# A two-layer hybrid encoder: down products of the second tokens held back, two token-major pairs, a third weight buffer set, and other places for the weight splits

## The chip, the cores and the metric

The kernel runs on one core of one Trainium2 chip. The metric is the device time of one execution in microseconds; what is compared is the median of several runs. One execution was also recorded by the hardware profiler; its page and its trace are what the text reads. The engines are called PE (TensorE, matrix products; its weight loads are shown apart as PEld), DVE (VectorE), ACT (ScalarE), POOL (GpSimd) and SP (SyncE, which here only issues DMAs).

## The reference

Two layers act on 256 tokens of width 1024 in float32. Each layer adds three sub-layers to the residual stream x, each with an RMS norm before it (pre) and after it (post):

```
for l in range(DEPTH):                                    # DEPTH = 2
    h = rmsnorm(x, ffn1_pre_g[l])
    x = x + 0.5 * rmsnorm(swiglu(h, ffn1_w_gate[l], ffn1_w_up[l], ffn1_w_down[l]), ffn1_post_g[l])
    h = rmsnorm(x, mix_pre_g[l])
    x = x + rmsnorm(hybrid_mixer(h, w_in[l], w_out[l], ...), mix_post_g[l])
    h = rmsnorm(x, ffn2_pre_g[l])
    x = x + 0.5 * rmsnorm(swiglu(h, ffn2_w_gate[l], ffn2_w_up[l], ffn2_w_down[l]), ffn2_post_g[l])

def swiglu(h, w_gate, w_up, w_down):
    return (silu(h @ w_gate) * (h @ w_up)) @ w_down       # 1024 -> 2816 -> 1024
```

The mixer projects h to 4 groups of heads (gated DeltaNet, differential attention, Mamba-2 SSD, mLSTM), and w_out maps their 1024 joined columns back. The change leaves the inside of the mixer as it is, apart from where weights lie.

## The kernel before, in words

**Six phases.** `phases` runs f1, mix, f2 of layer 0 and then of layer 1. Between two phases stands `boundary` (L512); one opens the first phase, one ends the last.

**Exact products from rounded parts.** Each float32 operand is split into hi (rounded by an ACT copy) and lo (a DVE subtraction), and a product is three matmuls: hi·hi, hi·lo, lo·hi. So each weight tile is loaded by SP as `raw` (L299), rounded by ACT into `hi` (L170) and subtracted by DVE into `lo` (L321). All weights of the program stand in one list, `stream`, in the order of use; it is worked through in halves of 512 KB. `split_to(n)` splits all halves up to n, `load_to` issues their loads, and `weights(i, ahead)` splits up to entry i plus `ahead` halves. There are 4 raw buffers and 8 split buffers, 4 in the pools `whi`/`wlo` ("w") and 4 in `ehi`/`elo` ("ext"); `room` says which half goes where, and `shifted` which are put 32 columns into their buffer. The mixer takes the place of "ext" while it runs.

**A feed-forward phase.** The 2816 columns are 11 pairs of 256 (`NPAIR`). For a pair, `project_T` computes gate and up transposed (weights stationary, all 256 tokens moving; 48 matmuls each), `swish` and `split_h` make the two parts of the hidden block, and two pairs later `contract` adds that pair's down product to four PSUM banks, one for each token half t (128 tokens) and output half h; each call is 6 matmuls of 512 columns. So a step of the loop is 96 matmuls of 256 columns and 24 of 512. The first pair of a phase is computed token-major by `ffn_first` (tokens stationary, `project`), so that it can start as soon as the 128 tokens of t = 0 are normed; its hidden block is turned by 4 transposes (`ps_hT`).

**The boundary.** For each t, `Norm` does: sum of squares of the bank (`junk_acc`, ACT), times the post gain (`ny`, DVE), the root (`rms_tail`: two small ACT and three small DVE instructions), the residual update (`x`, two DVE instructions), the sum of squares of x (`junk_x`), times the pre gain (half on DVE, half on POOL), the second root, the scaling (`ny`, DVE and ACT), 8 transposes (`flip`, PE, tile `ps_xT`), and the split into `xhi` and `xlo`. After t = 0 comes the first token-major work on t = 0, then the same chain for t = 1. All down products (or, after the mixer, all output products: `finish`) are issued before the boundary begins. The order is written out by hand (`manual_schedule`), and each engine works through its instructions in that order.

**The opening.** x, the identity, the first pre-norm gain spread over 128 partitions (512 KB, `gain_row`, L341) and the first weights are loaded, and the norms run without a post part.

## Time and profile before

| | before |
|---|---|
| median of 3 runs | 1195.69 us (1194.63 to 1198.77) |
| profiled execution | 1197.52 us, its span 1195.7 us |
| PE busy | 1120.7 us (94%) |
| DVE, ACT, POOL busy | 754.8, 580.2, 60.8 us |
| granted PE clock, mean | 0.970 |
| DMA | 189.64 MB, mean 159 GB/s |

The span runs from the first to the last recorded instruction; the execution's own time is 1.8 us longer. A busy share is an average over the phases, so it is read by place: in a steady loop an engine is either the bound or not, and at a boundary the question is which wait ends last. In the rows of the timeline the first number is the start and the second the duration in us; "idle before" names what the instruction waited for. In the rows by stretch come the length, then the busy time of each engine, the granted clock of PE, the share of the DMA engines and GB/s.

### The profile page before, as it was taken

What the parts mean: (1) busy time and instruction counts of PE and PEld (TensorE: products, weight loads), DVE (VectorE), ACT (ScalarE), POOL (GpSimd) and SP (SyncE); (2) the same over time, 40 slices, a digit from 0 to 9 for tenths busy, and PEclk for the clock granted to TensorE, in tenths of its full rate; (3) what the DMA queues carried; (4) which work ended last, traced back from release to release, by engine and by line L of the source; (5) the groups of instructions that cost most, each with busy time, mean ns of one, the idle gap of its engine ahead of it and who ended that gap; (6) DMA issues with size and microseconds to landing.
All of it is one profiled execution on the core that took longest, in us unless ns stands there. A gap on an engine that the chain in (4) does not pass through costs nothing.

```text
span 1195.7 us, 20955 instructions
## 1 busy us (share of the span) xinstructions
PE 1120.7 (94%) x8468; PEld 1039.9 (87%) x8468; DVE 754.8 (63%) x1306; ACT 580.2 (49%) x953; POOL 60.8 (5%) x76
## 2 busy tenths in 40 slices
PE   5999998999979889999989999989999798999997
PEld 4999897899968789999889999978998687999996
DVE  4655546877777865555476555477777677655535
ACT  5544536534344564544465444355335446544434
POOL 1000000010201000000000000001012010000000
PEclk9999999989989999999989999989899898999999
DMA  7866556322325466666447656454214243766642
GB/s 233 290 214 194 179 156 179 107 64 78 107 71 176 139 215 188 182 195 210 144 157 230 188 180 197 143 143 126 73 51 142 72 148 119 248 208 199 189 141 71
DMA packets 148851, 189.64 MB, mean 159 GB/s; under 512 B 12190, under 2 KB 133266, under 8 KB 148626
## 3 DMA queue, kind: packets, MB, share of 16 engines
q1 hardware_dynamic: 148754, 188.31, 50.4%
q8 instruction: 66, 1.08, 0.4%
q14 instruction: 31, 0.25, 0.1%
HBM read 187.24 MB, written 1.05 MB: 157 GB/s over the span
## 4 chain that ended last, share of the span: by engine, by line
PE 72%; DVE 11%; ACT 7%; DMA 6%; issue 3%; SPq 0%; POOL 0%; DVEq 0%; ACTq 0%
PE pgu L196 33%; PE acc L196 16%; DMA raw_d<-in_ffn_w_down 2%; PE ps_dq L196 2%; DMA raw_g<-in_ffn_w_gate 2%; PE ps_av L196 1%; PE ps_s L196 1%; PE ps_y L196 1%; PE ps_bq L196 1%; PE ps_dv L196 1%; PE ps_do L196 1%; PE ps_aq L196 1%; ACT hi_g L170 1%; PE ps_cz L196 1%; PE ps_ak L196 1%
## 5 line engine op out<-in xcount | busy, mean ns | idle before, releaser
L196 PE MATMUL pgu<-xhi,hi_g 128*128 128x256 f32 x640 | 178.4, 279 | 6.8 <-DVE hf L176 6.8
L196 PE MATMUL pgu<-xlo,hi_g 128*128 128x256 f32 x640 | 178.2, 278 | 0.0
L196 PE MATMUL pgu<-xhi,lo_g 128*128 128x256 f32 x640 | 177.9, 278 | 0.0
L196 PE MATMUL pgu<-xhi,hi_u 128*128 128x256 f32 x640 | 177.1, 277 | 0.0
L196 PE MATMUL pgu<-xhi,lo_u 128*128 128x256 f32 x640 | 176.9, 276 | 0.0
L196 PE MATMUL pgu<-xlo,hi_u 128*128 128x256 f32 x640 | 176.8, 276 | 0.0
L321 DVE TENSOR_TENSOR lo_u<-raw_u,hi_u 128x1024 fp32r<-128x1024 f32 x88 | 107.2, 1224 | 77.9 <-ACT hi_u L170 72.9
L321 DVE TENSOR_TENSOR lo_d<-raw_d,hi_d 128x1024 fp32r<-128x1024 f32 x88 | 104.6, 1222 | 64.1 <-ACT hi_d L170 63.5
L170 ACT ACTIVATE hi_u<-raw_u 128x1024 fp32r<-128x1024 f32 x88 | 92.7, 1060 | 95.6 <-PE pgu L196 87.2
L196 PE MATMUL acc<-hi_d,mlo 128*128 128x512 f32 x352 | 138.8, 394 | 0.0
L196 PE MATMUL acc<-lo_d,mhi 128*128 128x512 f32 x352 | 138.0, 392 | 0.0
L321 DVE TENSOR_TENSOR lo_g<-raw_g,hi_g 128x1024 fp32r<-128x1024 f32 x88 | 104.2, 1222 | 52.1 <-ACT hi_g L170 52.0
L196 PE MATMUL acc<-hi_d,mhi 128*128 128x512 f32 x352 | 136.8, 389 | 0.0
L196 PEld LDWEIGHTS pgu<-xhi,hi_g 128*128 128x128 f32 x640 | 120.7, 189 | 8.9 <-DVE hf L176 7.6
L196 PEld LDWEIGHTS pgu<-xlo,hi_g 128*128 128x128 f32 x640 | 120.8, 189 | 1.6
L196 PEld LDWEIGHTS pgu<-xhi,lo_g 128*128 128x128 f32 x640 | 120.9, 189 | 0.0
L196 PEld LDWEIGHTS pgu<-xhi,hi_u 128*128 128x128 f32 x640 | 120.2, 188 | 0.0
L196 PEld LDWEIGHTS pgu<-xlo,hi_u 128*128 128x128 f32 x640 | 120.1, 188 | 0.0
L196 PEld LDWEIGHTS pgu<-xhi,lo_u 128*128 128x128 f32 x640 | 120.1, 188 | 0.0
L170 ACT ACTIVATE hi_g<-raw_g 128x1024 fp32r<-128x1024 f32 x88 | 88.9, 1055 | 53.5 <-issue 36.9
L170 ACT ACTIVATE hi_d<-raw_d 128x1024 fp32r<-128x1024 f32 x88 | 88.9, 1049 | 52.3 <-PE pgu L196 34.1
L176 DVE TENSOR_TENSOR hf<-pgu,sg 128x256 f32<-128x256 f32 x88 | 36.8, 422 | 74.3 <-ACT sg L142 74.1
(494 smaller groups left out, 2355.7 us busy)
## 6 DMA issues: line engine op xcount, KB each, us to landing
raw_g<-in_ffn_w_gate SPq DMA_DIRECT2D x88, 512.0 KB
raw_u<-in_ffn_w_up SPq DMA_DIRECT2D x88, 512.0 KB
raw_d<-in_ffn_w_down SPq DMA_DIRECT2D x88, 512.0 KB
raw_wo<-in_w_out SPq DMA_DIRECT2D x16, 512.0 KB
raw_s<-in_w_in SPq DMA_DIRECT2D x4, 528.0 KB
g_ffn_pre_g<-in_ffn_pre_g SPq DMA_DIRECT2D x4, 512.0 KB
g_ffn_post_g<-in_ffn_post_g SPq DMA_DIRECT2D x4, 512.0 KB
raw_cz<-in_w_in SPq DMA_DIRECT2D x4, 512.0 KB
```

What stands on the lines that cost most here:

```text
L170: return nc.scalar.activation(out=out, in_=in_, func=AF.Copy, **kw)
L176: return (eng or V).tensor_tensor(out=out, in0=a, in1=b, op=op)
L196: return nc.tensor.matmul(out, lhsT=lhsT, rhs=rhs, start=start, stop=stop)
L321: V.tensor_sub(out=lo, in0=raw[:, 0:m], in1=hi.bitcast(F32))
```

## The change

1. **Down products held back.** In the loop the down products of pairs 7 and 8 (those of the last two steps) are done for t = 0 only. After the loop come pairs 9 and 10 for t = 0. The rest for t = 1 is passed to `boundary` as `tail`: pairs 7 and 8, and 9 and 10 for h = 0, are issued at its start (36 matmuls), pairs 9 and 10 for h = 1 (12 matmuls) after the transposes of t = 0. After the mixer the same is done with the output products of t = 1 (12 and 12).
2. **Two token-major pairs.** In all feed-forward phases but the first, `ffn_first` does pairs 0 and 1. At the boundary three of t = 0's four blocks (24 matmuls each) stand before the transposes of t = 1 and one behind; t = 1's four blocks follow. There are 8 transposes of hidden blocks in place of 4.
3. **Buffers.** A third set of 4 split buffers ("x2", pools `xhi`/`xlo`) exists outside the mixer, and there are 6 raw buffers in place of 4. `ROLES` gives each phase its sets for even pairs, odd pairs and down weights. The columns of the buffers, the paddings and `shifted` change with them, and the mixer's weights are no longer shifted.
4. **Places for splits.** Within a feed-forward phase splits run 6 halves ahead but not into the next phase. The first halves of the next phase are split before the boundary (4 between two feed-forward phases and before the mixer of layer 0, none before the mixer of layer 1, 2 after a mixer), and others at five points inside it (`fills`): around the residual update of t = 0, after its scaling, between the two halves of t = 1's post part, around t = 1's update, and after its scaling.
5. **Norms.** Both halves of x times the pre gain are on DVE, each behind its half's sum of squares; POOL has no part in it.
6. **The opening.** The first gain is loaded as one row of 4 KB into one partition and spread by two float32 matmuls with a row of ones; the norms read it from PSUM. The weight splits of the first pair are placed between the steps of the norms.

The core of the diff:

```diff
+RAW = 6
+AHEAD = 6
+ROLES = {(0, "f1"): ("w", "x2", "ext"), (0, "f2"): ("x2", "w", "ext"), (1, "f1"): ("x2", "ext", "w"), (1, "f2"): ("x2", "w", "ext")}
...
+    tpad = ctx.enter_context(tc.tile_pool(name="tpad", bufs=1))
+    tpad.tile([128, 104], F32, name="tskew")
...
-            nh = 2 * (len(stream) - c0)
+            shifted.update(2 * ids[l, st, "u", m] for m in range(1, NPAIR))
+            even, odd, down = ROLES[l, st]
             for m in range(NPAIR):
-                for nm in "gu":
-                    shifted.add(2 * ids[l, st, nm, m] + (m == 0))
-            for j in range(nh):
-                if j >= nh - 4:
-                    more = True
-                elif j >= nh - 6:
-                    more = False
-                else:
-                    more = j // 4 % 2 == 1
-                room[2 * c0 + j] = "ext" if more else "w"
+                where = odd if m % 2 else even
+                for nm in "gud":
+                    i = ids[l, st, nm, m]
+                    room[2 * i] = room[2 * i + 1] = where if nm != "d" else odd if m >= NPAIR - 2 else down
...
-                if n != "ak":
-                    shifted.add(2 * ids[l, n] + (n in ("cz", "do", "bv", "dv")))
...
+    def split_hi():
+        n = len(parts)
+        load_to(n + RAW - 1)
+        w, k2, _, name, _ = half_of(n)
+        m = w * k2
+        where = room.get(n)
+        if isinstance(where, tuple):
+            hi, lo = (ph.pools["early"].tile([128, 1024], F32R, tag=g, name=h + name) for g, h in zip(where, ("hi_", "lo_")))
+        elif where in ("ext", "x2"):
+            a, b = ("ehi", "elo") if where == "ext" else ("xhi", "xlo")
+            hi = ph.pools[a].tile([128, 1088], F32R, tag="hi", name="hi_" + name)
+            lo = ph.pools[b].tile([128, 1088], F32R, tag="lo", name="lo_" + name)
+        else:
+            hi = hip.tile([128, WMAX], F32R, tag="hi", name="hi_" + name)
+            lo = lop.tile([128, WMAX], F32R, tag="lo", name="lo_" + name)
+        o = 32 if n in shifted else 0
+        acopy(hi[:, o:o + m], raws[n][:, 0:m])
+        half_done.append((hi[:, o:o + m], lo[:, o:o + m]))
+    def split_lo():
+        n = len(parts)
+        w, k2, _, name, _ = half_of(n)
+        hi, lo = half_done.pop()
+        V.tensor_sub(out=lo, in0=raws[n][:, 0:w * k2], in1=hi.bitcast(F32))
+        parts.append(tuple(a.rearrange("p (k f) -> p k f", k=k2) for a in (hi, lo)))
+        load_to(n + RAW)
...
+    def weights(i, ahead=0, limit=NHALF):
+        split_to(max(2 * i + 1, min(2 * i + 1 + ahead, limit - 1)))
...
+    def first_gain_load(name, l):
+        V.memset(sall[0:1, 0, 0:128], 1.0)
+        nc.sync.dma_start(out=flat(npbd[0:1]), in_=t_in[name][l].rearrange("(o n) -> o n", o=1))
+
+    def first_gain():
+
+        ps = [psg("ps_gain%d" % h) for h in range(2)]
+        for h in range(2):
+            mm(ps[h][:], sall[0:1, 0, 0:128], flat(npbd[0:1])[:, 512 * h:512 * h + 512])
+        return ps
...
-            mul(self.y[:, HALF[0]], xt[t][:, HALF[0]], self.gpre[:, HALF[0]])
-            mul(self.y[:, HALF[1]], xt[t][:, HALF[1]], self.gpre[:, HALF[1]], eng=G)
+                mul(self.y[:, HALF[h]], xt[t][:, HALF[h]], self.gpre(h))
...
+        def amid(q):
+            def fill(what):
+                for c in fills[q][:1]:
+                    assert c == len(parts)
+                    split_hi() if what == "hi" else split_lo()
+            return fill
+        def after(q):
+            for c in fills[q]:
+                assert c == len(parts)
+                split_to(c)
+        for h in range(2):
+            n[0].acc_ss(h)
+            n[0].acc_y(h)
+        n[0].update(amid(0) if nxt else None)
         if not nxt:
             nc.sync.dma_start(out=out_d[0, 0:128, :], in_=xt[0])
-            n[1].acc(0)
-            n[1].acc(1)
+            for part in tail[1:]:
+                part()
+            for h in range(2):
+                n[1].acc_ss(h)
+                n[1].acc_y(h)
             n[1].update()
             nc.sync.dma_start(out=out_d[0, 128:256, :], in_=xt[1])
             return
         n[0].scale()
+        after(1)
         n[0].flip()
-        if accs:
-            n[1].acc(0)
-        n[0].parts(0)
-        if accs:
-            n[1].acc_ss(1)
-            n[1].acc_y(1)
-        n[0].parts(1)
-        first(0)
-        if accs:
-            n[1].update()
+        for part in tail[1:]:
+            part()
+        n[0].parts()
+        n[1].acc_ss(0)
+        n[1].acc_y(0)
+        first = firsts_of(nxt)
+        after(2)
+        n[1].acc_ss(1)
+        n[1].acc_y(1)
+        n[1].update(amid(3))
         n[1].scale()
+        after(4)
+        for piece in first[:3]:
+            piece(0)
         n[1].flip()
-        n[1].parts(0)
-        n[1].parts(1)
-
-    def starts(phase):
+        for piece in first[3:]:
+            piece(0)
+        n[1].parts()
...
+    def opening(nxt):
+        gs = first_gain()
+        n = [Norm(t, None, None, 1.0, lambda h: gs[h][:]) for t in range(2)]
+        first = firsts_of(nxt, 1)
+        n[0].scale()
+        split_to(0)
+        n[0].flip()
+        n[0].parts()
+        split_to(1)
+        n[1].scale()
+        first[0](0)
+        n[1].flip()
+        if nxt[1] == "mix":
+            n[1].parts()
+            first[1](0)
+        else:
+            split_to(2)
+            n[1].parts()
+            split_to(3)
+            first[1](0)
+            first[0](1)
+            first[1](1)
...
+        return [lambda t, c=c, m=m: ffn_first(l, st, t, c, m) for m in range(pairs) for c in "gu"]
...
+        if c == "g":
+            heads_of[t, m] = (psg if t else psa)("pgu")
+        o = 256 * (c == "u")
+        project(weights(ids[l, st, c, m]), t, heads_of[t, m][:, o:o + 256], 256)
...
+        if pairs > 1:
+            for piece in firsts_of((l, st)):
+                piece(1)
+        hs = t1024([128, 2, 2, 256], "h0")
+        for t in range(2):
+            split_to(2 * ids[l, st, "gu"[t], pairs] + 1)
+            for m in range(pairs):
+                swish(heads_of[t, m][:, 0:256], heads_of[t, m][:, 256:512], hs[:, t, m, :])
...
+                for t in range(2 if m < NPAIR - 2 else 1):
                     for h in range(2):
                         contract(acc, t, h, w, 2 * ((m - 2) % 4), m == 2, False)
         table("natural_log_exp_and_others")
-        ws = [(m, weights(ids[l, st, "d", m], 6 - 2 * n)) for n, m in enumerate((NPAIR - 2, NPAIR - 1))]
-        for t in range(2):
-            for h in range(2):
-                for m, w in ws:
-                    contract(acc, t, h, w, 2 * (m % 4), False, m == NPAIR - 1)
-        boundary(acc, gains[p + "_post_g", l], 0.5, nxt)
+        ws = {m: weights(ids[l, st, "d", m]) for m in range(NPAIR - 4, NPAIR)}
+        fills = ((), (), (), (), ())
+        c = limit
+        if nxt and nxt[1] != "mix":
+            split_to(c + 3)
+            fills = ((c + 4,), (c + 5,), (c + 6,), (c + 7,), ())
+        elif nxt and ROLES[l, st][2] != "w":
+            split_to(c + 3)
+        elif nxt:
+            fills = ((c,), (c + 1,), (c + 2, c + 3), (), ())
+        def down(t, ms, hs):
+            for h in hs:
+                for m in ms:
+                    contract(acc, t, h, ws[m], 2 * (m % 4), False, m == NPAIR - 1)
+        a, b = (NPAIR - 4, NPAIR - 3), (NPAIR - 2, NPAIR - 1)
+        down(0, b, (0, 1))
+        def tail():
+            for m in a:
+                down(1, (m,), (0, 1))
+            down(1, b, (0,))
+        boundary(acc, gains[p + "_post_g", l], 0.5, nxt, (tail, lambda: down(1, b, (1,))), fills)
...
+            ph.open("xhi", "xlo", bufs=4)
+            c = 2 * ids[l, "f2", "g", 0]
+            split_to(c + 1)
+            fills = ((c + 2,), (c + 3,), (c + 4, c + 5), (c + 6,), (c + 7,))
+        boundary(accs, gains["mix_post_g", l], 1.0, nxt, last(), fills)
...
+            def out(t, h):
+                for m, w in list(zip(ms, ws))[1 - t:]:
+                    contract(accs, t, h, w, 2 * m, False, m == ms[1])
+            out(0, 0)
+            out(0, 1)
+            return (lambda: out(1, 0)), (lambda: out(1, 1))
```

More of the change, by code (lines that the diff above doesn't have):

```diff
@@ L589, in ffn @@
             for q in range(2):
                 project_T(wg, q, ps[q][:, 0:SEQ])
[L591 removed]
+            if m == pairs:
                 for t in range(2):
[L593 to L597 removed]
@@ L598, in ffn @@
-            wu = weights(ids[l, st, "u", m], 6)
+                    for n in range(pairs):
+                        pt = psb("ps_hT")
+                        for q in range(2):
+                            nc.tensor.transpose(pt[:, 128 * q:128 * q + 128], hs[:, t, n, 128 * q:128 * q + 128], ident)
+                        sl = slice(128 * t, 128 * t + 128)
+                        split_psum(mhi[:, 2 * n:2 * n + 2, sl], mlo[:, 2 * n:2 * n + 2, sl],
+                                   pt[:, 0:256].rearrange("p (q c) -> p q c", q=2))
@@ L843, in splits @@
         def splits():
[L844 removed]
+            last = 2 * ids[l, "wo", WO_ORDER[3]] + 1
             for n in range(2 * ids[l, "ak"] + 2, last + 1):
```

144 lines of the change are left out of this document (55 added, 89 removed).

## The prediction

> **What bounds the kernel now.** I read the page first, then the chain of waits in order of time, then stretches around each boundary.
>
> ```profile
> PE 1120.7 (94%) x8468; PEld 1039.9 (87%) x8468; DVE 754.8 (63%) x1306; ACT 580.2 (49%) x953; POOL 60.8 (5%) x76
> PE   5999998999979889999989999989999798999997
> ```
>
> PE is busy everywhere but in a few slices, so only those can give time. The chain shows the steady loop, a disturbed step, and the end:
>
> ```profile
> 457.52 10.95 PE pgu L196 x96
> 468.47 5.50 PE acc L196 x24
> ...
> 439.39 12.64 PE pgu L196 x96
> ...
> 1172.25 16.50 PE acc L196 x72
> ```
>
> A step is 96 matmuls of 256 columns at 0.114 us and 24 of 512 at 0.229 us, without a gap: 16.45 us. The changed loop has the same matmuls, so nothing is won there. The stretches from the last product of a phase until the next loop runs, in order of time (A f1 to mixer, B mixer to f2, C f2 to f1, D f1 to mixer, E mixer to f2), then three shorter ones:
>
> ```profile
> 205.00:226.00 21.00, 16.49 (x118) 15.50 (x118) 15.60 (x35) 12.46 (x30) 2.56 (x2) 0.92 0.16 47
> 404.50:446.00 41.50, 33.99 (x258) 32.70 (x258) 29.33 (x48) 26.02 (x46) 2.55 (x2) 0.92 0.54 178
> 600.00:636.00 36.00, 30.39 (x230) 29.24 (x230) 26.74 (x47) 23.77 (x44) 2.90 (x2) 0.91 0.52 172
> 793.00:814.00 21.00, 16.88 (x108) 15.71 (x108) 15.57 (x35) 12.12 (x29) 2.54 (x2) 0.84 0.12 35
> 995.00:1031.00 36.00, 29.68 (x227) 28.34 (x226) 27.46 (x48) 23.10 (x43) 2.56 (x2) 0.91 0.48 159
> 610.00:636.00 26.00, 24.11 (x203) 23.47 (x202) 18.55 (x25) 17.27 (x27) 0.99 (x1) 1.00 0.63 209
> 436.00:439.40 3.40, 0.72 (x8) 0.53 (x6) 1.84 (x3) 1.36 (x3) 0.00 (x0) 0.93 0.99 336
> 439.40:445.00 5.60, 5.60 (x36) 5.60 (x37) 3.55 (x5) 2.97 (x5) 0.00 (x0) 0.73 0.58 169
> ```
>
> What a stretch loses is its length less PE's busy time, plus length times (1 - granted clock). A: 4.5 + 1.7 = 6.2 us; B: 7.5 + 3.3 = 10.8; C: 5.6 + 3.2 = 8.8; D: 4.1 + 3.4 = 7.5; E: 6.3 + 3.2 = 9.5. Sum 42.8. The slow clock follows the pauses: after the one of 2.7 us in 436 to 439.4 it costs 5.6 x 0.27 = 1.5 and 0.2 before, 1.7 in all; in 610 to 636 the pauses are of 1.4 us and less, and the clock is 1.00. I take 1.7 to 3.4 us (A, D), middle 2.55, for each pause over 2.7 us, and nothing for those under 1.5.
>
> The pause itself is the norm chain. For C:
>
> ```profile
> 595.67 0.57 ACT L413 ACTIVATE junk_acc<-acc 128x512 f32<-128x512 f32 x1
> 600.12 0.63 ACT L413 ACTIVATE junk_x<-x 128x512 f32<-128x512 f32 x1 [1.53 <-DVE x L190]
> 601.31 1.62 POOL L176 TENSOR_TENSOR ny<-x,g_ffn_pre_g 128x512 f32<-128x512 f32 x1 [185.75 <-DVE pre_v L186]
> 603.81 1.94 PE L477 MATMUL ps_xT<-cst,ny 128*128 128x128 f32 x8 [3.72 <-DVE ny L186]
> ...
> 1183.33 0.60 ACT L413 ACTIVATE junk_acc<-acc 128x512 f32<-128x512 f32 x1 [2.06 <-PE acc L196]
> 1185.56 1.42 DVE L190 SCALAR_TENSOR_TENSOR x<-ny,nr,x 128x512 f32<-128x512 f32 x2
> ```
>
> From a bank's end to half of x takes 1185.56 + 0.71 - 1183.33 = 2.9, with the hand-over 3.0 us (from the last boundary, where ACT was free); from there to the transposes 603.81 - 600.12 = 3.7. So the chain is 6.7 us. Now it has the 24 products of t = 1 as cover (5.5 us), and ACT comes to it late.
>
> **Part 1, held products.** Call 0 the end of t = 0's banks. After an FFN, 36 matmuls follow: 36 x 0.229 = 8.25 us of cover against 6.7. After a mixer 12 follow: 2.75 us. The number of matmuls is unchanged.
>
> **Parts 4 and 5, splits in the chain.** The splits and the shared multiplication:
>
> ```profile
> L321 DVE TENSOR_TENSOR lo_u<-raw_u,hi_u 128x1024 fp32r<-128x1024 f32 x88 | 107.2, 1224 | 77.9 <-ACT hi_u L170 72.9
> L170 ACT ACTIVATE hi_u<-raw_u 128x1024 fp32r<-128x1024 f32 x88 | 92.7, 1060 | 95.6 <-PE pgu L196 87.2
> ...
> 601.13 0.68 DVE L176 TENSOR_TENSOR ny<-x,g_ffn_pre_g 128x512 f32<-128x512 f32 x1
> ...
> 609.92 1.62 DVE L176 TENSOR_TENSOR ny<-x,g_ffn_pre_g 128x512 f32<-128x512 f32 x1
> 217.78 1.04 PE L477 MATMUL ps_xT<-cst,ny 128*128 128x128 f32 x8
> ...
> 219.80 3.06 PE ps_s L196 x22
> ```
>
> A fill is 1.06 us on ACT, mostly in ACT's free time, and 1.22 us on DVE in the middle of the chain: with hand-over 1.35 us per fill. It waits behind nothing else: its raw is loaded 6 halves before, and the buffer it takes is free once pair 7 of t = 1 is through (2.75 us, when ACT gets there). Taking POOL out adds 0.68 us to DVE and removes the stretching of DVE's own half from 0.68 to 1.62 us: 0, bounds -0.9 to +0.7 per chain.
>
> A (no fill, four halves split ahead: DVE 4 x 1.22 = 4.9 us, done 0.9 after 0): chain 7.6 under 8.25, no pause. Then transposes 1.05 and 12 products until 12.05. t = 1's chain ends at 12.05 + 6.7 = 18.75; PE has s and cz, 48 matmuls at 0.118, until 17.7. Pause 1.0, and 1.0 after the flip as now (219.80 - 217.78 - 1.04). Lost 2.0; won 4.2.
>
> C (fill in the chain): 0.9 + 6.7 + 1.35 = 9.0, pause 0.75. For t = 1 three fills: 6.7 + 3 x 1.35 less some 1.1 that lies under the 12 products = 9.65, against three token-major blocks of 24 x 0.114 = 8.2: pause 1.4. Lost 2.2 plus part 2.
>
> D (fill, none ahead): 8.05 under 8.25. For t = 1, ACT and DVE have three splits, two of them between the halves of its post part: 9.9 against s and cz, 5.7: pause 4.2, slow clock 2.55, 1.0 after the flip. Lost 7.75; won -0.2.
>
> B and E: chain 6.7 + 1.35 = 8.05, under 2.75: pause 5.3, slow clock 2.55; t = 1: 9.3 against 8.2, 1.1; the last fill is after the scaling and PE meets its lo 0.5 late. Lost 9.45 plus part 2.
>
> [...]
>
> **Part 2, two pairs.** The matmuls are as many; 4 transposes more are 4 x 1.04 / 8 = 0.5 us, and the fourth `ps_hT` waits for the first of three banks to be emptied, 0.45 us. What it removes: the pauses in the first loop step (2.7 us in B, 1.4 in C) sit in the losses of now, since splits queued ahead of `swish` wait there for DMA; with 6 raw buffers and the first 8 halves split inside the boundary I count none. So C loses 3.2 (won 5.6), B and E 10.4 each (won 0.4 and -0.9).
>
> **Part 3, buffers.** In the loop splits will run earlier; PE does not wait for them now, so 0. One use is tighter: pairs 9 and 10 of t = 0 come 2.75 us sooner, at 583.43 + 12 x 0.229 + 6 x 0.229 = 587.55 for pair 10. Its hidden block was ready at 591.0 (below), as ACT stood waiting for a DMA. With the raw loaded 6 halves ahead ACT is free and it is ready 2 us after the last up product (583.4): 0, bound +3.4 per FFN.
>
> ```profile
> 583.43 0.39 PE L196 MATMUL acc<-hi_d,mhi 128*128 128x512 f32 x1
> ...
> 586.20 1.06 ACT L170 ACTIVATE hi_d<-raw_d 128x1024 fp32r<-128x1024 f32 x1 [2.59 <-DMA raw_d<-in_ffn_w_down]
> 587.16 0.37 ACT L142 ACTIVATE sg<-pgu 128x256 f32<-128x256 f32 x1
> ...
> 590.58 0.42 DVE L575 TENSOR_TENSOR mlo<-hf,mhi 128x256 fp32r<-128x256 f32 x1 [0.48 <-ACT mhi L170]
> ```
>
> **Part 6, opening.**
>
> ```profile
> 4.29 0.63 ACT L413 ACTIVATE junk_x<-x 128x512 f32<-128x512 f32 x1 [2.28 <-DMA x<-in_x]
> 8.58 0.69 DVE L176 TENSOR_TENSOR ny<-x,g_ffn_pre_g 128x512 f32<-128x512 f32 x1 [3.20 <-DMA g_ffn_pre_g<-in_ffn_pre_g]
> 11.18 1.97 PE L477 MATMUL ps_xT<-cst,ny 128*128 128x128 f32 x8 [11.18 <-DVE ny L186]
> ...
> L196 PE MATMUL ps_D<-gcm,cst 128*128 128x512 f32 x8 | 3.8, 592 | 0.0
> ...
> 43.73 0.39 PE L196 MATMUL pgu<-xhi,hi_g 128*128 128x256 f32 x1 [1.49 <-DVE hf L176]
> ```
>
> DVE waits 3.2 us for the gain. The row of 4 KB lands about with x (4.3); spreading a half takes two passes of 0.59 us, nearer 1.2 cold, so the second is in PSUM at 6.5 to 9; after it 0.7 + 0.75 + 0.5 us: transposes at 8.5 to 11, I take 9.6, 1.6 us sooner. The pause of 1.5 us at 43.73 should go; splits placed between the norms cost about 0.6 (u waits for its lo). Won 2.5, bounds 0 to 4.5. The last boundary ends as now: its last 12 products and t = 1's chain are the same.
>
> **Sum.** 4.2 + 0.4 + 5.6 - 0.2 - 0.9 + 2.5 = 11.6 us. The profiled execution took 1197.5 us, so 1185.9; that one lies 1.8 above the median, and the forecast against the median is 1195.7 - 11.6 = 1184 us. Its own range: opening 0 to 4.5, four chains by -0.9 to +0.7, slow clock by 0.85 three times: 1178 to 1190.
>
> **Rivals.**
> Clock kept: the pauses of B, D and E bring no slow stretch: 3 x 2.55 less, 1176. For it: pauses of up to 1.5 us cost nothing; against: 2.7 us did. [...]
> Chains late: at A and C the fills or the four splits ahead push the chain 2 us beyond its cover and the clock drops: 2 x (2 + 2.55) more, 1193. For it: DVE is already 0.9 late there; against: 1.6 us of room in A.
> Not what it says: t = 0's last products wait for pair 10 as ACT does now, 3.4 us in four FFNs, 13.6 in all: 1198. For it: the DMA wait quoted; against: two more raw buffers.
> Slower: the places of the operands. The shifts and paddings change for all 640 x 6 + 64 x 6 = 4224 gate and up matmuls; steps of matmuls of this size differ at full clock:
>
> ```profile
> 231.29 2.77 PE ps_aq L196 x24
> 234.87 2.94 PE ps_aq L196 x24
> ```
>
> 0.115 and 0.1225 us, both above the loop's 0.114. From 0.1177 on (3.6 us x 4224 / 1000 = 15.2 us) it is slower than before by 0.3%; at 0.120 it is 4224 x 0.006 = 25 us, 1209. For it: 0.1225 exists; against: all PE rows of the loop agree while the buffers rotate.
>
> **Chances.** Forecast 0.54, clock kept 0.18, chains late 0.11, not what it says 0.09, slower 0.08. A difference of 0.3% (3.6 us) is about what a measurement of this kernel can tell from none. Faster: the first two and half of "late", 0.77; the same: the other half and "not what it says", 0.14; slower 0.09. Range 1172 to 1195, to both of the nearer rivals.
>
> **What would show it.** Right: PE's pause before the first transposes under 1 us at A, C and D and near 5 us after the mixers; `ps_xT` at full clock in A and C; no wait for `hf` in the first loop step; POOL out of the boundaries. Wrong: `acc` waiting for `mhi` after the loop, ACT waiting for a DMA or a buffer inside a boundary, or a loop step above 11.1 us for its 96 matmuls.

## The result, and the profile after

The changed kernel takes 1168.45 us (median of 4 executions, 1166.11 to 1169.04) against 1195.68 us for the kernel before: ratio 0.976, 95% interval 0.973 to 0.979. The forecast was 1184 us, with a range of 1172 to 1195. The direction was right; the gain is 27.2 us where 11.6 were forecast, and the time lies below the range. A second series of the same kernel, run beside some of the experiments, gave 1166.22 us, ratio 0.976 (0.974 to 0.978).

The page of the profiled execution (1166.11 us, span 1164.3) has these lines for TensorE and GpSimd, and the slices of TensorE and its clock:

```profile
PE 1111.1 (95%) x8484; PEld 1031.8 (89%) x8484; DVE 742.7 (64%) x1319; ACT 569.1 (49%) x953; POOL 43.9 (4%) x64
PE   7999999899979899999999999999998898999997
PEclk9999999989989999999999999998999898999999
```

PE's busy time fell by 9.6 us and the span by 31.4. The matmul count went up by 16, the added transposes and the spreading of the gain; matmuls that run at half clock count as longer (of 256 columns 0.41 us at 241.5, where the granted clock is 0.50, and 0.28 at 234), so that part of the busy time is the clock.

The view by stretches, over the opening and the five boundaries (A, B, C, D, E in this order, opening last; columns as before):

```profile
188.00:217.00 29.00, 27.86 (x176) 24.81 (x175) 20.92 (x48) 16.01 (x37) 0.00 (x0) 1.00 0.34 104
384.00:444.00 60.00, 54.82 (x393) 51.30 (x392) 45.04 (x75) 39.86 (x69) 0.00 (x0) 0.97 0.63 200
572.00:628.00 56.00, 55.50 (x398) 51.79 (x397) 40.75 (x70) 35.41 (x63) 0.00 (x0) 1.00 0.61 193
758.00:788.00 30.00, 27.25 (x175) 24.37 (x175) 22.36 (x49) 18.96 (x40) 0.00 (x0) 1.00 0.36 104
954.00:1016.00 62.00, 56.81 (x397) 52.82 (x396) 45.65 (x75) 40.14 (x69) 0.00 (x0) 0.94 0.60 187
0.00:57.00 57.00, 49.30 (x338) 44.27 (x339) 36.80 (x57) 36.01 (x55) 1.62 (x6) 1.00 0.84 287
```

Length less PE's busy time, plus length times (1 - clock): A loses 1.1 us, B 5.2 + 1.8 = 7.0, C 0.5, D 2.8, E 5.2 + 3.7 = 8.9. Together 20.3 us, where 42.8 were lost before. C is nearly free of loss, and A and D run at full clock in this execution. The 1.00 of the opening is not to be taken at its word: the clock's record begins at 17.1 us, and before it the first 8 transposes take 1.97 us, later ones 1.04.

The waits of TensorE and ScalarE, after and then before (in all, how often, the longest):

```profile
PE ps_xT L500 <- DVE ny L193: 14.3, 5, 4.7
ACT hi_u L177 <- DMA raw_u<-in_ffn_w_up: 0.9, 2, 0.7
```

```profile
PE ps_xT L477 <- DVE ny L186: 30.4, 7, 11.2
PE pgu L196 <- DVE hf L176: 6.8, 4, 2.7
ACT hi_d L170 <- DMA raw_d<-in_ffn_w_down: 18.2, 13, 2.6
ACT hi_g L170 <- DMA raw_g<-in_ffn_w_gate: 9.4, 8, 2.5
ACT hi_u L170 <- DMA raw_u<-in_ffn_w_up: 5.4, 12, 1.1
```

Three things went: a part of TensorE's wait for the normed rows, all of its wait for `hf` in the first loop steps, and nearly all of ScalarE's 33 us of waiting for weights to land. In the first, the opening weighs heavily: its one wait is 11.2 us before and 1.95 after, as TensorE now has the gain to spread in between; without it 19.2 us became 12.4. The prediction gave the last no term of its own. The chain of waits after shows the loop's step (96 matmuls in 10.91 us, before 10.95):

```profile
443.29 10.91 PE pgu L203 x96
```

To place the gain I use four kinds of marks in TensorE's order that both kernels have: the end of the first down products of each FFN, the first product of `ps_ak`, the last `ps_mo` of each mixer, and the last product. Times between marks, before less after, in us; each row holds a boundary with the loop steps next to it. The second column of measurements is a second profile of the changed kernel, and the last column a kernel that appears below, the one before with six raw buffers alone.

| stretch | forecast | measured | second profile | six raw buffers alone |
|---|---|---|---|---|
| opening | 2.5 | 3.4 | 3.0 | 0.8 |
| f1, A | 4.2 | 5.7 | 5.4 | 2.3 |
| mixer | 0 | 0.8 | 0.1 | -1.1 |
| B | 0.4 | 4.3 | 3.5 | 3.6 |
| f2, C | 5.6 | 8.5 | 8.9 | 4.4 |
| f1, D | -0.2 | 5.0 | 4.1 | 3.3 |
| mixer | 0 | 2.5 | 2.2 | 1.8 |
| E | -0.9 | 0.8 | 2.3 | 2.9 |
| f2, end | 0 | 0.4 | 0.4 | 0.0 |
| sum | 11.6 | 31.4 | 29.8 | 17.9 |

The profiled execution of before lay 1.8 us above its median and the first of after 2.3 below; the medians differ by 27.2.

### The profile page after: what moved, and what is told of

It reads as the page before. It is cut to its first block, busy times and chain, and to the rows that moved or that the text cites. A ratio compares the mean times of both kernels' runs of the same rounds, so it can differ in the third digit from the quotient of the medians.

```text
span 1164.3 us, 20842 instructions
## 1 busy us (share of the span) xinstructions
PE 1111.1 (95%) x8484; PEld 1031.8 (89%) x8484; DVE 742.7 (64%) x1319; ACT 569.1 (49%) x953; POOL 43.9 (4%) x64
## 3 DMA queue, kind: packets, MB, share of 16 engines
q8 instruction: 66, 1.08, 0.4%
## 4 chain that ended last, share of the span: by engine, by line
PE 80%; DVE 11%; ACT 4%; issue 3%; POOL 1%; DMA 0%; DVEq 0%; SPq 0%; ACTq 0%; POOLq 0%
PE pgu L203 41%; PE acc L203 20%; PE wo L203 3%; PE ps_dq L203 2%; PE ps_av L203 1%; DVE gQ L183 1%; PE ps_dv L203 1%; PE ps_aq L203 1%; PE ps_ak L203 1%; PE ps_sc L203 1%; PE ps_bq L203 1%; PE ps_xT L500 1%; DVE ny L183 1%; PE ps_do L203 1%; PE ps_gr L203 1%
## 5 line engine op out<-in xcount | busy, mean ns | idle before, releaser
L149 ACT ACTIVATE sg<-pgu 128x256 f32<-128x256 f32 x88 | 33.5, 384 | 267.9 <-PE pgu L203 267.7
L203 PE MATMUL pgu<-xhi,hi_g 128*128 128x256 f32 x592 | 164.0, 277 | 0.0
L203 PE MATMUL pgu<-xhi,hi_u 128*128 128x256 f32 x592 | 163.9, 277 | 0.0
L203 PE MATMUL pgu<-xlo,hi_g 128*128 128x256 f32 x592 | 163.8, 277 | 0.0
L203 PE MATMUL pgu<-xhi,lo_g 128*128 128x256 f32 x592 | 163.6, 276 | 0.0
L203 PE MATMUL pgu<-xhi,lo_u 128*128 128x256 f32 x592 | 163.6, 276 | 0.0
L203 PE MATMUL pgu<-xlo,hi_u 128*128 128x256 f32 x592 | 163.6, 276 | 0.0
L183 DVE TENSOR_TENSOR hf<-pgu,sg 128x256 f32<-128x256 f32 x74 | 31.4, 425 | 197.4 <-ACT sg L149 197.3
L203 PEld LDWEIGHTS pgu<-xlo,hi_g 128*128 128x128 f32 x592 | 111.3, 188 | 1.4
L203 PEld LDWEIGHTS pgu<-xhi,hi_g 128*128 128x128 f32 x592 | 111.2, 188 | 1.3
L203 PEld LDWEIGHTS pgu<-xhi,lo_g 128*128 128x128 f32 x592 | 111.2, 188 | 0.0
```

What stands on the lines that cost most here:

```text
L149: return nc.scalar.activation(out=out, in_=in_, func=func, **kw)
L183: return (eng or V).tensor_tensor(out=out, in0=a, in1=b, op=op)
L203: return nc.tensor.matmul(out, lhsT=lhsT, rhs=rhs, start=start, stop=stop)
```

## The experiments

Unless said otherwise, each kernel is the changed one with one edit, and its median stands against 1168.45 (first series) or 1166.22 us (second). Ratios are to the kernel before in the same series; its median lay between 1195.4 and 1198.2 us in the series, so that a difference of under 3 us between medians of two series is not resolved.

### Products not held back after the FFNs

```diff
-                for t in range(2 if m < NPAIR - 2 else 1):
+                for t in range(2):
...
-        boundary(acc, gains[p + "_post_g", l], 0.5, nxt, (tail, lambda: down(1, b, (1,))), fills)
+        boundary(acc, gains[p + "_post_g", l], 0.5, nxt, (lambda: down(1, b, (0, 1)),), fills)
```

> The changed kernel with the held products undone after the four FFN phases: the loop again does both token halves of pairs 7 and 8, and all 24 remaining products of the second half stand ahead of the first transposes. Theory (the boundary is priced by cover: products between the end of t = 0's banks and the transposes): t = 0's chain took about 7.4 us in the changed kernel, its cover falls from 8.25 to 5.5 us, so pauses of about 1.9 us come back before the transposes at A, C and D, about 1.2 us after them, and the pauses of 0.7 (A) and 2.3 us (D) before the second transposes go. Together +6 to +7 us, 1175; should the three pauses reach 2.7 us and bring slow clock, up to +14, 1182. Rival (the gain came from buffers, loads and operand places, not from the order of the products): within 2 us of the changed kernel, 1167 to 1170.

Measured: 1184.79 us, ratio 0.991 (0.989 to 0.994), 16 us more. Between the marks A took 2.7 us more (162.1 against 159.4), C 6.2 (190.8 against 184.6), D 7.0 (166.0 against 159.0). TensorE's rows at C and D:

```profile
592.72 1.15 PE L500 MATMUL ps_xT<-cst,ny 128*128 128x128 f32 x8 [2.00 <-DVE ny L193]
783.64 1.06 PE L500 MATMUL ps_xT<-cst,ny 128*128 128x128 f32 x8 [2.08 <-DVE ny L193]
796.09 1.06 PE L500 MATMUL ps_xT<-cst,ny 128*128 128x128 f32 x8 [1.32 <-DVE ny L193]
```

At C and D the pauses are the 1.9 us that the theory gave (at A 1.08), but they were enough to halve the clock. It is halved in windows of 3.41 us (last section), and each costs up to 1.7 us: two at C, 3.4 us, and two and one at D, 3.4 and 1.7 us. That puts the result beyond the upper end. The pause before D's second transposes, which was to go, is 1.32 us. The rival falls. With everything else of the change kept, this kernel is no faster than the one with six raw buffers alone (below, ratio 0.985, 0.982 to 0.989): without the held products, the rest of the change brings nothing on top of the buffers.

### One token-major pair

```diff
-        if pairs > 1:
-            for piece in firsts_of((l, st)):
+        if (l, st) != phases[0]:
+            for piece in firsts_of((l, st), pairs):
...
-        first = firsts_of(nxt)
+        first = firsts_of(nxt, 1)
...
-                ffn(l, st, nxt, 1 if (l, st) == phases[0] else 2)
+                ffn(l, st, nxt, 1)
```

> The changed kernel with one token-major pair in every FFN, as before, all else kept (eight halves still split inside the boundary). In B, C and E the second half's chain is covered by two blocks of 24 matmuls in place of three, 2.75 us less, and four transposes and a wait of 0.5 us fall away. Theory (cover): pauses of about 2.3 us before the second transposes in C, and up to that in B and E, about 4 us in all, and up to as much again where such a pause brings slow clock: 1172 to 1177; no wait for hf in the first loop step, as six raw buffers and the splits inside the boundary keep ScalarE free. Rival (the forecast's: the pair removed the pauses of 2.7, 1.4 and 1.2 us of the first loop step, no more): those come back as waits of the first down products for hf, and the pauses before the second transposes do not: 1168.5 + 5.3 - 2.9 = 1171.

Measured: 1182.68 us, ratio 0.987 (0.986 to 0.989), 14 us more, beyond both. The pauses before the second transposes stand where the theory put them, in B, C and E:

```profile
412.83 1.07 PE L500 MATMUL ps_xT<-cst,ny 128*128 128x128 f32 x8 [2.00 <-DVE ny L193]
602.93 1.06 PE L500 MATMUL ps_xT<-cst,ny 128*128 128x128 f32 x8 [2.54 <-DVE ny L193]
992.77 1.06 PE L500 MATMUL ps_xT<-cst,ny 128*128 128x128 f32 x8 [2.00 <-DVE ny L193]
```

No wait for `hf` came back, so the rival falls: with the loads ahead the pair is not what removes it. B took 5.9, C 1.9 and E 4.7 us more between marks than in the first profile; behind each 2.00 us pause the clock was halved for two windows, 3.4 us each. The second pair's worth is the cover it lays over the second half's chain.

### Four raw buffers

```diff
-RAW = 6
+RAW = 4
```

> The changed kernel with four raw buffers in place of six. Theory (the order of work decides, not the loads): 0 to 2 us more, 1168.5 to 1170.5, all of it in waits of ScalarE for a raw tile inside or just behind the boundaries. Rival (the loads: six buffers keep ScalarE from standing at a DMA, which before cost the pauses of the first loop steps and 3.4 us at the last hidden block): 5 us and more, 1173.5 or later, with pauses before acc or hf.

Measured: 1175.68 us, ratio 0.981 (0.979 to 0.983), 7.2 us more. The amount fits the rival, the place only in part: some 5 us are lost in the opening, to one wait for `hf` and a slow window behind it (1.7 us), while the stretches of A to D take what they take in the second profile, to 0.1 us; the first mixer takes 1.7 us more and E 1.5.

```profile
44.11 0.58 PE L203 MATMUL pgu<-xhi,hi_g 128*128 128x256 f32 x1 [2.86 <-DVE hf L183]
```

ScalarE's waits for weights come back, 121 us of them where the kernel before had 33, and yet they hardly reach the boundaries. That the three buffer sets and the splits laid into the boundaries keep them off the chain is likely, but was not tried:

```profile
ACT hi_u L177 <- DMA raw_u<-in_ffn_w_up: 103.4, 62, 3.2
ACT hi_d L177 <- DMA raw_d<-in_ffn_w_down: 14.7, 9, 2.0
```

### Six raw buffers alone, in the kernel before

```diff
-    rawp = ctx.enter_context(tc.tile_pool(name="raw", bufs=4))
+    rawp = ctx.enter_context(tc.tile_pool(name="raw", bufs=6))
...
-    RAW, AHEAD = 4, 2
+    RAW, AHEAD = 6, 2
```

> The kernel before with six raw buffers in place of four and nothing else of the change (its second buffer set takes 1088 words a buffer in place of 1152, and the DMA scratch is halved, to make room). Theory (of 27 us the loads carry some 7, as taking them back cost 7.2): the waits of the first loop steps for hf, 1.5 us in the opening, 2.7 in B, 1.4 in C, 1.2 in E, shrink or go, the slow stretch behind the one in B too: 5 to 8 us less than before, 1187 to 1190. Rival (the loads bring something only together with the splits inside the boundary; in the kernel before the splits queue up ahead of swish whatever the loads do): 0 to 2 us less, 1193 to 1195.5, with the waits for hf in their place.

Measured: 1178.76 us against 1198.17 for the kernel before beside it, ratio 0.985 (0.982 to 0.989): 17 to 19 us less, by the two medians of the kernel before (1195.7 and 1198.2). That is more than twice the theory and far from the rival. The narrower buffers do not speed up the loop: from the last mark but one to the last it takes 142.56 us, as before. No wait for `hf` is left, which the theory had; but the pauses before the first transposes shrink too, which it had not:

```profile
205.78 0.41 PE L477 MATMUL ps_xT<-cst,ny 128*128 128x128 f32 x2 [1.49 <-DVE ny L186]
406.04 1.09 PE L477 MATMUL ps_xT<-cst,ny 128*128 128x128 f32 x8 [3.43 <-DVE ny L186]
595.68 1.06 PE L477 MATMUL ps_xT<-cst,ny 128*128 128x128 f32 x8 [1.19 <-DVE ny L186]
784.71 1.06 PE L477 MATMUL ps_xT<-cst,ny 128*128 128x128 f32 x8 [1.49 <-DVE ny L186]
```

At C the pause was 3.72 us before (the prediction shows the row), at A and D:

```profile
208.40 1.07 PE L477 MATMUL ps_xT<-cst,ny 128*128 128x128 f32 x8 [3.30 <-DVE ny L186]
796.39 1.06 PE L477 MATMUL ps_xT<-cst,ny 128*128 128x128 f32 x8 [3.21 <-DVE ny L186]
```

Why, is seen on ScalarE at C. First the kernel before:

```profile
582.54 1.06 ACT L170 ACTIVATE hi_d<-raw_d 128x1024 fp32r<-128x1024 f32 x1 [1.45 <-DMA raw_d<-in_ffn_w_down]
586.20 1.06 ACT L170 ACTIVATE hi_d<-raw_d 128x1024 fp32r<-128x1024 f32 x1 [2.59 <-DMA raw_d<-in_ffn_w_down]
...
596.24 0.59 ACT L413 ACTIVATE junk_acc<-acc 128x512 f32<-128x512 f32 x1
```

and with six raw buffers:

```profile
575.41 2.00 ACT L170 ACTIVATE hi_d<-raw_d 128x1024 fp32r<-128x1024 f32 x2
...
589.10 0.60 ACT L413 ACTIVATE junk_acc<-acc 128x512 f32<-128x512 f32 x1 [1.86 <-PE acc L196]
```

Before, ScalarE stood 1.45 + 2.59 us at weights that had not landed, in the last loop step; everything queued behind came late, and the square sum of t = 0's second bank started at 596.24, when that bank had been complete since 583.43 + 48 x 0.229 = 594.4. ScalarE never waited for TensorE there. With six buffers it stands waiting for the bank (1.86 us) and starts when it is complete: 1.8 us of chain are gone, and of the two slow windows behind the pause one is left. In the whole profile there are 16 slow windows in place of 21, TensorE's waits for the normed rows fall from 30.4 to 23.9 us, and the 6.8 us of waiting for `hf` are gone.

### The old opening

```diff
-        first_gain_load(PRE[st], l)
+        gain(PRE[st], l)
...
-        gs = first_gain()
-        n = [Norm(t, None, None, 1.0, lambda h: gs[h][:]) for t in range(2)]
+        gs = gains[PRE[nxt[1]], nxt[0]]
+        n = [Norm(t, None, None, 1.0, lambda h: gs[:, HALF[h]]) for t in range(2)]
```

> The changed kernel with the first gain loaded as 128 rows again (512 KB) and no spreading by TensorE; the order of splits between the two first norms stays as changed. Theory: the first transposes come at about 11.2 us in place of 9.8 (as before), so 1.4 us more, 1169.9; the other 2 us of the 3.4 won in the opening came from the order of the splits and from the first loop step's wait, and stay. Rival (all of the opening's gain hangs on the gain row): 3.4 us more, 1171.9. Second rival: no change, because the wait moves to the weights' landing.

Measured: 1168.71 us, ratio 0.975 (0.973 to 0.978), which cannot be told from the changed kernel. In the profile the first transposes come at 11.11 us, with the spread gain at 9.83, and the first mark at 58.46 against 57.02 and 57.40: 1.1 to 1.4 us, as the theory had it, and too little for this series to show in the median.

```profile
11.11 1.97 PE L500 MATMUL ps_xT<-cst,ny 128*128 128x128 f32 x8 [11.11 <-DVE ny L193]
```

```profile
9.83 1.97 PE L500 MATMUL ps_xT<-cst,ny 128*128 128x128 f32 x8 [1.95 <-DVE ny L193]
```

The other 2 us of the opening are not the gain row's. The wait for `hf`, 1.49 us before, is a part of them and comes back with four raw buffers (above); six raw buffers alone shorten the opening by only 0.8 us. TensorE also leaves its slow start, with matmuls of 256 columns at 0.41 us, one every 0.21, in place of 0.28, one every 0.12, at 17.1 and 17.0 us in the two profiles of the changed kernel, at 19.1 before and at 21.2 with six buffers alone: two us at about half that rate are one us of work. What the order of the splits does was not tried by itself.

### GpSimd in the multiplication again

```diff
-                mul(self.y[:, HALF[h]], xt[t][:, HALF[h]], self.gpre(h))
+                mul(self.y[:, HALF[h]], xt[t][:, HALF[h]], self.gpre(h), eng=G if h and self.accs else None)
```

> The changed kernel with GpSimd doing the second half of the multiplication by the pre-norm vector in the eight norms of the boundaries, as before (the opening stays on VectorE). Theory: GpSimd takes 1.62 us beside a VectorE stretched to as much, against 1.28 us for both halves on VectorE: 0.35 us more per exposed chain, four of them exposed (B and E before the first transposes, A and D before the second), 1.4 us more: 1170. Rival (the forecast's lower bound: 0.9 us per chain): 3 to 4 us more, and the pauses at C and D come back and bring slow clock. Second rival (its upper bound: VectorE gains 0.7 us per chain): 2 to 3 us less.

Measured: 1174.88 us, ratio 0.981 (0.978 to 0.983), 6.4 us more. The pauses grew by 0.3 (A), 0.2 (B, E) and 0.6 us (D), 1.3 in sum as the theory had it:

```profile
398.52 1.73 PE L500 MATMUL ps_xT<-cst,ny 128*128 128x128 f32 x7 [4.91 <-DVE ny L193]
782.79 1.51 PE L500 MATMUL ps_xT<-cst,ny 128*128 128x128 f32 x6 [2.89 <-DVE ny L193]
```

This profile has 18 slow windows of 3.41 us where the two of the changed kernel have 14 and 15, so slow clock, 1.7 us a window, makes up the larger part of the difference there. Whether the longer pauses bring that many more on average, four executions don't settle.

### After the mixers: all 24 products ahead of the transposes

```diff
-            return (lambda: out(1, 0)), (lambda: out(1, 1))
+            return (lambda: (out(1, 0), out(1, 1)),)
```

> The changed kernel, but after the two mixers the 12 products of the second half that stood behind the first transposes stand ahead of them again (24 ahead, 0 behind). Theory (cover, and a slow clock that follows long pauses): the 4.7 us pauses before the transposes fall to about 1.95 us, about 1.3 us of waiting for the split of the transposed block comes behind, and the slow stretches of 1.7 and 3.4 us after the two boundaries go: 2 x 1.4 + 5.1 = 8 us less, 1160. Rival 1 (the slow stretches come whatever the pause): 3 us less, 1165.5. Rival 2 (the forecast on record, by which the order after the mixers cost 0.9 us against before because t = 1's chain is late): 1 to 2 us less.

Measured: 1169.85 us, ratio 0.979 (0.974 to 0.984): no gain, and the theory's 8 us are refuted. The pauses are the expected ones, but behind both the clock was halved for two windows (3.4 us), while behind the 4.7 us pauses of the changed kernel it is one window or two:

```profile
398.80 1.07 PE L500 MATMUL ps_xT<-cst,ny 128*128 128x128 f32 x8 [1.95 <-DVE ny L193]
401.75 0.58 PE L203 MATMUL pgu<-hi_g,xlo 128*128 128x256 f32 x1 [0.81 <-DVE xlo L510]
973.01 1.06 PE L500 MATMUL ps_xT<-cst,ny 128*128 128x128 f32 x8 [1.94 <-DVE ny L193]
```

### The pauses after the mixers filled

```diff
+        if nxt and nxt[1] == "f2":
+            idle = psb("ps_idle")
+            for _ in range(16):
+                mm(idle[:], mhi[:, 0, 0:128], mhi[:, 0:2, :].rearrange("p k c -> p (k c)"))
```

> The changed kernel with 16 matmuls of 512 columns (3.7 us) added in each of the two 4.7 us pauses after the mixers; their result is not used. The path is not shortened: the chain on ScalarE and VectorE ends when it did. Theory (a slow clock of one or two stretches of 3.4 us follows a TensorE pause of over 2.5 us): the stretches at 395 to 400 and 965 to 973 go and with them 1.7 + 3.4 = 5.1 us: 1163. Rival (the stretches belong to something else, as the load of the mixer or a fixed grid): no change, 1168.5, or slower by what the added matmuls delay.

Measured: 1167.13 us, ratio 0.977 (0.972 to 0.982). The slow windows after both mixers are gone, as the theory says, and the 5 us are not won: pauses come up before the second transposes that were not there, at B and just so at E.

```profile
412.06 1.06 PE L500 MATMUL ps_xT<-cst,ny 128*128 128x128 f32 x8 [0.91 <-DVE ny L193]
```

With the slow clock, TensorE was late at its three blocks and the second half's chain hidden behind it, so slow clock and the next pause do not add up. Between marks B and E take 58.0 us each here; in the two profiles of the changed kernel they take 58.2 and 58.3 where one slow window falls into them, 59.1 and 59.7 where two do. One slow window of 1.7 us cost 0.2 us there, two cost 1.1 to 1.7.

### More products held back in the mixers

```diff
-                for t in range(2 if n < 2 else 1):
+                for t in range(2 if n < 1 else 1):
...
-            ms = WO_ORDER[2:]
+            ms = WO_ORDER[1:]
...
+            def tail():
+                for m in ms[:2]:
+                    for h in range(2):
+                        out(1, h, m)
+                out(1, 0, ms[2])
```

> The changed kernel, and in the two mixers the second half's 12 output products of the second head group are held back too: 36 products of t = 1 follow t = 0's banks (30 ahead of the transposes, 6 behind), as after an FFN. Theory: the 4.7 us pauses fall to 0.7 us; the last mixing block's transposes stand 2.9 us earlier in TensorE's order and may cost a pause of 0.5 to 0.9 us there; net 3.2 us per mixer, and the slow stretches of 1.7 and 3.4 us go: 11.5 us less, 1157. Rival 1 (slow stretches come whatever the pause): 6.4 us less, 1162. Rival 2 (the work is only moved: the mixer's end is bound by VectorE and the held products had filled its gaps): within 2 us of the changed kernel.

Measured: 1164.05 us, ratio 0.974 (0.968 to 0.979), 4.4 us less, between the rivals. Against the second series it is 2.2 us, and the intervals of the ratios overlap; the size of the gain is open.

```profile
397.63 1.06 PE L500 MATMUL ps_xT<-cst,ny 128*128 128x128 f32 x8 [0.61 <-DVE ny L193]
410.84 1.06 PE L500 MATMUL ps_xT<-cst,ny 128*128 128x128 f32 x8 [1.75 <-DVE ny L193]
```

The first pauses fall to 0.6 us and no slow window follows in B or E. What is given back is a new pause of 1.75 us before the second transposes. That t = 1's chain now begins at once behind t = 0's, with VectorE's three splits in it, is the likely reason; it was not tried.

### Matmuls added where TensorE waits in the mixers and at D

```diff
+    def busy(p, src, n):
+        for _ in range(n):
+            mm(p[:], src[:, 0, 0:128], src[:, 0:2, :].rearrange("p k c -> p (k c)"))
...
             pt = psb("ps_am")
+            busy(pt, xhi, 8)
...
+                if (t, half, a) == (1, 0, 0):
+                    busy(ps, xhi, 12)
...
+                if h == 0 and late:
+                    busy(p, mhi, 6)
```

The first of these kernels is the changed one repeated, as the measure.

> The changed kernel once more, as the measure for the other kernels of this call. Theory (the slow clock comes in windows of 3.41 us on a grid whose phase is another in every execution, and a window in which TensorE was busy for less than about half is followed by a slow one): the same pauses as in the first profile (4.68, 2.29, 4.69 us), but another number of slow windows behind them, 1.7 us of time each; median 1167 to 1171. Rival (the slow stretches belong to places of the program): slow stretches at the same places and of the same lengths as in the first profile, none at D.

> The changed kernel, with matmuls added whose result is not used, in pauses that TensorE spends waiting for VectorE: 8 of 512 columns before ps_am (pause 2.51 us) and 12 before the first ps_sc (3.33 us) in each mixer, 6 before the second transposes of D (2.29 us). No chain is shortened. Theory (windows under half busy bring the slow ones): behind ps_am one slow window of 1.7 us goes where it came, behind ps_sc one to three of the three in each mixer, at D one or two where they came: 5 to 9 us less than the changed kernel, 1160 to 1163; the two slow windows that follow ps_gr (64 x 64 matmuls, no pause) stay. Rival (slow stretches belong to places of the program): no change, or up to 1 us more.

> The changed kernel with 36 products of t = 1 held back after the mixers and with the added matmuls of the run before in the mixers and at D. Theory: both gains, 4.4 us from the held products (as measured) and 5 to 9 from the clock: 1155 to 1159. Rival: the held products' gain alone, 1164.

Measured: 1166.22 us for the changed kernel, 1166.24 with the added matmuls, ratio 0.975 (0.973 to 0.978), and 1163.07 with these and the products held in the mixers, ratio 0.970 (0.967 to 0.973). The changed kernel repeated has the pauses of the first profile (4.69, 2.30, 4.69 us), but two slow windows at B for one, one at E for two and one at D for none; its median is a little under the theory's, and the rival of fixed places falls.

The added matmuls removed three of the mixers' ten slow windows, and the mixers together took 338.9 us between marks against 338.2 and 337.1 in the two profiles of the changed kernel; so the theory's gain there is refuted. At D the pause fell to 0.8 us and no slow window followed, in both kernels. With the pause of 2.3 us one followed in five of eight profiles, not in the first of the changed kernel; D took 158.9 us, against 159.9 in the second profile, which had one, and 159.0 in the first. In the mixer, time given back turns into another wait, here for ScalarE (0.67 us at this place in the second profile of the changed kernel):

```profile
347.11 1.10 PE L203 MATMUL ps_bo<-bv,bpe 128*128 128x64 f32 x8 [1.87 <-ACT bpe L177]
```

The last of the three is 3.2 us below both in the median, near its rival's 1164 and not in the theory's range, so no gain from the clock is shown. Its five executions lie between 1155.66 and 1166.58, the slowest inside the range of the changed kernel, and the intervals of the ratios just touch (0.967 to 0.973 against 0.973 to 0.978). The two fastest, at 1155.7 and 1156.4 us, had a mean granted clock of 0.99, the slowest 0.98.

## Why the prediction was too small

**What bounds the kernel, and the chain.** Right. The forecast built the boundaries from a chain of 6.7 us from t = 0's banks to the transposes, the time that it takes when ScalarE is free. The kernel with six raw buffers shows it bare at C: 595.68 less the bank's end, 577.85 + 48 x 0.229 = 588.8, is 6.8 us.

**The step that failed: the price of a split in the chain (Parts 4 and 5).** The pauses before the transposes that the forecast left add up to 20.2 us (A 1.0, B and E 5.3 + 1.1 each, C 0.75 + 1.4, D 4.2); the first profile has 12.4 (0.68, 4.68, none, 2.30, 4.69). The forecast lengthened each chain by 1.35 us per split. With one split the chain took 7.4 us at B (2.75 of cover and the pause), and 7.5 and 7.6 at C and D in the kernel without held products (5.5 + 2.00 and 5.5 + 2.08); the forecast had 8.05 to 9.0. With three it took 8.2 us at D (from the last product at 771.0 to 779.16, forecast 9.9), and 8.0 at C in the kernel with one pair (5.5 + 2.54, forecast 9.65). The split costs less because its halves fall into gaps: at B ScalarE does its half (390.47 to 391.51) while VectorE is at the reciprocal root, and VectorE's half (392.63 to 393.85) overlaps ScalarE's second square sum. At B half of x is there at 392.09:

```profile
392.09 0.63 ACT L437 ACTIVATE junk_x<-x 128x512 f32<-128x512 f32 x1 [0.57 <-DVE x L197]
```

From there to the transposes (396.61) it is 4.5 us with a split and without GpSimd, against the 3.7 of before: 0.8 for Parts 4 and 5 together. Taking GpSimd out was within the bounds set for it: putting it back made an exposed chain 0.2 to 0.6 us longer.

**What else the sum had too high.** The wait behind the second transposes (1.0 at A and D, 0.5 at B and E) came to 0.9 us in all and not 3.0. Slow clock was charged with 7.65 us at B, D and E; it was 5.1 in the first profile and 6.8 in the second. At B and E the forecast added a second pause of 1.1 us to the slow clock; the pause was there (0.91) only when the slow clock was gone, so the overlap was wrong, not the chain. Pauses, waits and clock make up some 12 us of the 19.8 by which the first profile beats the forecast, mixers, loop and opening some 6 (below); the rest is not assigned. A sum in it is wrong too, without weight for the result: its own range adds up to 1176 to 1192, not 1178 to 1190.

**The term put at nothing: Part 3, buffers.** Here the forecast had the cause wrong. It quoted the row on which this turned (586.20, ScalarE waiting 2.59 us for `raw_d`) and used it only for a rival. It wrote that ScalarE "comes to it late" in the kernel before, and did not ask why. Its chains of 6.7 us already have a ScalarE that is not late, and Part 2 counts no wait for `hf` "with 6 raw buffers", so the cure is in its sum, booked under the held products and the pair; this 0 alone does not make the sum too small. But the loads alone are worth 17 to 19 us, more than the whole forecast: chain (1.8 us at C), the four waits for `hf` (6.8 us), and the slow clock behind both. In the changed kernel four raw buffers cost only 7 us; the likely reading is that loads, third buffer set and splits inside the boundary are remedies of one lateness, but the latter two were not taken back by themselves. From the six-buffer kernel to the changed one another 11 us are won (1178.8 to 1167), and the held products and the second pair must both be there for it: without the one it is 1184.8, without the other 1182.7, and neither is faster than the six buffers alone (by the ratios the second cannot be told from them, 0.987 against 0.985).

**Part 1, held products.** Right in kind: no pause before the first transposes at A, C and D, and 4.7 us after the mixers where 5.3 were forecast:

```profile
396.61 0.66 PE L500 MATMUL ps_xT<-cst,ny 128*128 128x128 f32 x2 [4.68 <-DVE ny L193]
767.20 1.04 PE L500 MATMUL ps_xT<-cst,ny 128*128 128x128 f32 x8
779.16 1.07 PE L500 MATMUL ps_xT<-cst,ny 128*128 128x128 f32 x8 [2.30 <-DVE ny L193]
```

**The slow clock.** 2.55 us were charged to each pause over 2.7 us, and nothing below 1.5. The length of a pause is not what decides: pauses of 2.0 us halved the clock for two windows, 3.4 us of loss (the kernels without held products and with one pair), the one of 2.3 at D did or did not, in two executions of the same kernel, and that of 4.7 at B cost 1.7 in the first and 3.4 in the second. The rival "clock kept" was right for D in the first profile, by luck of the grid (below), and wrong for B and E.

**Part 2.** The four added transposes cost 0.5 us in B, C and E and the wait behind them 0.5, as forecast. But the end of the wait for `hf` was booked under the pair, though the loads bring it, and the pair's cover was taken for granted in the other terms; it decides 14 us.

**Part 6.** Near in size: 3.0 to 3.4 us for 2.5, the first transposes at 9.83 where 9.6 was forecast. The gain row's share is 1.1 to 1.4 of the 1.6 forecast; some 1 us is the earlier end of the slow start, which no term held.

**What no term held.** The mixers gave 2.3 to 3.4 us in all. Most of it is in the second, which had six slow windows before and five in both profiles of the changed kernel. Over the profiles, it takes 170.4 to 172.2 us with six and 167.9 to 169.3 with five, the six-buffer kernel among the latter; so this is the count of slow windows and no work of the change that the runs show. The loop's step is 0.05 us shorter, under 2 us over some 36 steps, so that the operand places, if it is they, went the other way from the rival "slower". Pair 10's block was not late: TensorE's products run on without a pause after the loop. The chains were not late at A and C.

## What to carry to other kernels

When an engine off the critical path comes late to the work that is on it, ask what it was waiting for just before, and cost the cure of that by itself: here two more load buffers alone won 17 to 19 us, and all the rest of the change on top of them another 11. What is put into a chain can cost less than its own length, where it falls into the gaps of its engines, so read the gaps before pricing it: here chains with one split took 7.4 to 7.6 us, where 8.05 to 9.0 were forecast. Price cover as a set, since a part that lengthens a chain may pay only together with the part that covers it (here 14 and 16 us came back without the second pair or the held products), and a slow clock and the next pause can hide one another (one slow window of 1.7 us cost 0.2 us between the marks of B and E). Where single executions differ by two or three slow windows, judge an edit of 5 us by repeated medians, and not by one profile.

## What the runs showed of the clock

All slow stretches, in all profiles, begin on a grid of 3.413 us that runs on from the start of the recording to its end, with another phase in every execution. D is the same code with the same pause of 2.3 us in two executions of the changed kernel. The rows by stretch, cut on that grid, in the first profile:

```profile
774.84:778.26 3.42, 2.02 (x18) 1.82 (x16) 3.15 (x8) 1.98 (x6) 0.00 (x0) 1.00 0.66 217
778.26:781.67 3.41, 2.06 (x13) 1.63 (x14) 1.90 (x5) 2.57 (x4) 0.00 (x0) 1.00 0.00 0
```

and in the second:

```profile
778.21:781.63 3.42, 1.12 (x11) 0.94 (x10) 2.37 (x8) 1.84 (x6) 0.00 (x0) 1.00 0.24 86
781.63:785.04 3.41, 3.39 (x15) 2.76 (x14) 2.56 (x4) 3.05 (x4) 0.00 (x0) 0.50 0.00 0
```

In the first, the pause lies across two windows, TensorE is busy for 2.0 us in each, and the clock stays. In the second it falls into one, 1.1 us busy, and the next window runs at half clock. Over the 14 profiles of this study, outside the mixers (from the first `ps_ak` to the last `ps_mo`), after the first 25 us and without the windows from the last product on, 38 windows at full clock had TensorE busy for less than 0.48 of their length, and the next was slow each time; of 6 between 0.48 and 0.53 one was followed by a slow one, and of 19 between 0.55 and 0.7 none. A slow window that was itself busy for up to 0.76 was followed by a second one, 19 times of 19; one busy for 0.9 or more never, in 34; between these it went either way. So 2.0 us of pause can bring 3.4 us of slow clock, and 4.7 us only 1.7:

```profile
392.55:395.96 3.41, 0.00 (x0) 0.00 (x0) 3.22 (x9) 1.51 (x6) 0.00 (x0) 1.00 0.30 69
395.96:399.38 3.42, 2.77 (x11) 2.61 (x12) 2.19 (x3) 3.06 (x5) 0.00 (x0) 0.50 0.34 117
962.58:965.99 3.41, 0.00 (x0) 0.00 (x0) 3.27 (x8) 1.81 (x6) 0.00 (x0) 1.00 0.29 81
965.99:969.40 3.41, 2.46 (x10) 2.40 (x11) 2.13 (x5) 2.75 (x4) 0.00 (x0) 0.50 0.39 134
```

At B (first two rows) the slow window was busy for 2.77 of 3.42 us and the clock came back; at E (last two) for 2.46, and a second slow one followed.

In the mixers it is not so: once in each mixer of all 14 profiles, slow windows follow one in which TensorE has no pause. In the first profile that is 235.54 to 238.95, with TensorE busy for all 3.41 us and the granted clock at 0.50 in the next window, and it holds matmuls of 2 columns (`ps_ss`) and of 64 x 64 (`ps_gr`). Whether these matmuls bring the slow windows was not tried by itself.
